# One more Strassen pair in each feed-forward block, the row of 1/rms by products with ones, and weights split in the middle of the unit ahead

## The chip, the cores and the metric

The kernel runs on one core of a Trainium2 chip. The metric is device time in microseconds (us) of one execution; of several executions the median is given. The core has five engines with a queue each: TensorE (PE in the profile; PEld is its weight load), VectorE (DVE), ScalarE (ACT), GpSimd (POOL) and SyncE (SP), which here only issues transfers. Each engine works its queue in order and waits on semaphores for the others.

## The reference

The reference is a two-layer encoder trunk on 512 tokens of 1024 values, in float32. Each layer is a pre-norm attention block and a pre-norm SwiGLU feed-forward block with 2816 inner values:

```python
def rmsnorm(x, g):
    y = x32 * lax.rsqrt(jnp.mean(x32 * x32, axis=-1, keepdims=True) + RMS_EPS)
    return (y * g.astype(jnp.float32)).astype(x.dtype)
...
def swiglu(h, w_gate, w_up, w_down):
    return (jax.nn.silu(h @ w_gate) * (h @ w_up)) @ w_down
...
for i in range(DEPTH):
    h = rmsnorm(x, norm_mix[i])
    x = x + (window_gqa_sink(...) if i % 2 == 0 else dilated_mixture_attention(...))
    h = rmsnorm(x, norm_ffn[i])
    x = x + swiglu(h, w_gate[i], w_up[i], w_down[i])
return rmsnorm(x, norm_final)
```

Layer 0 has windowed attention with grouped queries and a sink logit, layer 1 dilated attention in three groups.

## The kernel before

The activations lie transposed in SBUF: `x` is eight tiles of 128 features by 512 tokens. A float32 product is made of three products of a rounded type (float32r): each operand is split into a high part (a copy that rounds, on ScalarE, `wh`, `xh`) and a low part (the difference, on VectorE, `wl`, `xl`), and `mm3` adds high x high, high x low and low x high into a PSUM bank. A *unit* is 128 output features: eight steps j of six products of 128x256, 48 in all. Its weights come in one transfer of 512 KB and are split by `load` (L104 to L108); three buffers of weights are in flight.

The norm isn't applied to the inputs of a unit. The products run on `x` times the gain, and 1/rms of each token is multiplied in when a result leaves PSUM. The sum of squares (`ssum`) is gathered tile by tile on GpSimd (L273). Then `norm_sums` (L296) adds it over the partitions with four products with a column of ones (`ssq`), and root, reciprocal and one Newton step run on a tile of 128x4 (`norm_columns`); `norm_rows` (L305) turns the result into a row of 512 that is the same in all partitions (`rrow`, four transposes) and copies it to `rb`.

In layer 0 (L345 to L493) attention units are woven with the units of q, k and the output projection by `fill`, a chain of generators: a unit there begins by loading and splitting its own weights, and its products follow.

The feed-forward block `swiglu` (L586) has 22 pairs of units, gate f and up f. The first `plain` of them (six) are ordinary units, in `conventional` (L863). `gated(f)` (L616) scales gate by `rb` and takes Silu, `combined(f)` scales up and multiplies, `kept(f)` splits the result for the down projection. The other pairs are *Strassen pairs*: gate and up of one pair, with the tokens in two halves and the features in two halves, form a 2x2 by 2x2 block product that is done with seven products of half the length (`strassen`, L717), each of 12 products of 128x256. They need seven inputs, normed and then added and subtracted, as high and low parts (`bh`, `bl`), and seven weights. The inputs are made by the 19 steps of `input_steps` (L633): eight `normed`, then `parts` (a split: ScalarE, then VectorE) and `less` (a difference on VectorE). `conventional` calls these steps one by one between the units of the plain pairs; their last pair also makes the weights of the first Strassen pair (`weights`, L681: h12, l12, f5 and so on). In `strassens` (L767) the Strassen pairs follow each other in turns of seven; between the products stand the copies (L726) that take a partial result out of a bank before more is added to it.

Who sets the order: TensorE's queue is in the order of the program text everywhere; in `conventional` and `strassens` (under `manual_schedule` with `ORDERED`) so are those of VectorE and ScalarE. Elsewhere a scheduler orders the other engines when the program is built.

Of the kernel before, what the change touches and what calls it, by code (L numbers as in the profile page):

```python
# [9 lines left out]
F32 = mybir.dt.float32  # L10
# [4 lines left out]
S = 512  # L15
# [51 lines left out]
def trunk(ctx, tc, xT, gains, sink, tabs, qsc, wunits, wv, outT, outR):  # L67
# [85 lines left out]
    def run(gen):  # L153
        for _ in gen:
            pass

    def chain(*gens):
        for _, g in gens:
            yield from g
# [18 lines left out]
    def lined_up(*makers):  # L178
# [5 lines left out]
        for k in range(len(makers)):  # L184
            n, gen = gens[k]
            for c in range(n):
# [3 lines left out]
                    next(gens[-1][1])  # L190
                yield

    def last_outputs(out_part, at, fill=()):

        gens = [out_part(j, at, NK)[1] for j in range(3)]
        for j in range(NK):
            run(gens[j])
            if j + 3 < NK:
                gens.append(out_part(j + 3, 0, NK, ahead=True)[1])
                next(gens[-1])  # L200
            if j == 0:
                run(fill)
# [102 lines left out]
    def norm_rows(blocks=range(4), at=0):  # L305

        r = norm["r"]
        pr = bank("tp", "rrow")
        for b in blocks:
            nc.tensor.transpose(pr[:, 128 * b:128 * b + 128], r[:, at + b:at + b + 1].to_broadcast([128, 128]), ident)  # L310
        rb = norm["rb"] = spool.tile([128, S], F32, name="rb", bufs=1)
        cols = slice(128 * blocks[0], 128 * blocks[-1] + 128)
        nc.scalar.activation(rb[:, cols], pr[:, cols], AF.Copy)
        for done in norm["wait"] or ():
            done()
        norm["wait"] = None
# [32 lines left out]
    with tc.tile_pool(name="l0", bufs=2) as pool:  # L349
# [121 lines left out]
        def out_part(j, lo, hi, w={}, ahead=False):  # L471
            def gen():
# [6 lines left out]
                for c in range(lo, hi):  # L479
                    mm3(out_ps[j], wh[:, c], wl[:, c], oh[:, c, :], ol[:, c, :], c == 0, c == NK - 1)  # L480
                    if c == NK - 1:
# [4 lines left out]

        early = values(0, 0, xh, xl, v0, "ov sc tp mm")[1]
        spread([norm_sums, 4, norm_rows], early)
        fill = chain((16, early), q_unit(0, 2), q_unit(0, 3), k_unit(1),
                     *[q_unit(1, i) for i in range(4)],  # L490
                     *[out_part(j, 0, 4) for j in range(3)], *[out_part(j, 4, 6) for j in range(3)])

        counts = [6, 7, 6, 5, 5, 5, 4, 4, 4, 4, 3, 2, 2, 2, 3, 2]  # L493
        units = [attention0(P, h, b) for P in range(2) for h in range(2) for b in range(4)]
# [90 lines left out]
    def swiglu(u, n):  # L585
        with tc.tile_pool(name="ffn", bufs=2) as pool:  # L586
# [24 lines left out]
            def up(f):  # L611
                def done(ps):
                    part["u"] = ps
                return unit(u0 + 2 * f + 1, xh, xl, ("tp", "mm")[f % 2], done)
# [238 lines left out]
                return (raws.pop(f), *sums_of.pop(f))  # L853

            ORDERED = {mybir.EngineType.PE, mybir.EngineType.DVE, mybir.EngineType.Activation}
            plain = 6
            parts = PARTS[n // 4]
            run(gate(0)[1])
            norm_sums()
            run(up(0)[1])  # L860
            steps = input_steps()

            def conventional():  # L863

                def products(ps, w):
                    for j in range(NK):
                        mm3(ps, w[0][:, j], w[1][:, j], xh[:, j, :], xl[:, j, :], j == 0, j == NK - 1)
                        yield

                def make(m):  # L870
                    for _ in range(m):
                        if steps:
                            steps.pop(0)()

                w = load_unit(wunits[u0 + 2], (NK, 128))
                for f in range(1, plain):
                    g = bank(("mm", "sc")[f % 2])
                    gen = products(g, w)
                    for q in range(4):
                        next(gen), next(gen)  # L880
                        if q == 0:
                            w = load_unit(wunits[u0 + 2 * f + 1], (NK, 128))
                            if f == 1:
                                norm_rows()
                                gated(0)
                            combined(f - 1)
                            part["g"] = g
                        elif q == 2 and f <= 3:
                            kept(f - 1)
                        elif q:  # L890
                            make(1)
                    ps = bank(("tp", "mm")[f % 2])
                    gen = products(ps, w)
                    for q in range(4):
                        if q < 3 or f < plain - 1:
                            next(gen), next(gen)
                        if f == plain - 1:
                            if q == 0:
                                first, parts_ = weights(*ready(f + 1))
                                ahead(f + 2)  # L900
                            for m in (("h12", "l12", "f5"), ("h64", "l64", "f7"), ("h57", "l57"), ("h3", "l3"))[q]:
                                parts_[m]()
                        if q == 3 and plain - 3 <= f < plain - 1:
                            ahead(f + 3, raw=False)
                        if q == 0 and f + 1 < plain:
                            w = load_unit(wunits[u0 + 2 * f + 2], (NK, 128))
                        if q == 0:
                            gated(f)
                        else:
                            make(2 if q == 2 and f < 3 else 1)  # L910
                    part["u"] = ps
                make(len(steps))
                return first, gen
# [505 lines left out]
```

## Time and profile before

| | us |
| --- | --- |
| median of 3 runs (lowest, highest) | 1396.22 (1395.93, 1396.76) |
| profiled execution | 1396.07 |
| its span, first to last instruction | 1394.3 |
| PE busy, x12414 | 1382.5 |
| DVE busy, x1593 | 855.4 |
| ACT busy, x1250 | 681.9 |
| POOL busy, x318 | 225.2 |

The mean granted clock of TensorE is 0.998. The first feed-forward block begins its gate 0 near 182 us, its Strassen pairs at 247.87; the second repeats it some 862 us later. In the profile a row of a time line is start, duration, engine, line, operation, what it writes and reads, shape and count; in brackets the idle time before it and what ended that. Products overlap in TensorE, so that the duration of one is longer than the distance between two.

### The profile page before, as it was taken

How to read it: one execution, taken by the hardware profiler on the slowest of the kernel's cores; microseconds unless marked ns; L12 is line 12 of the kernel's file. 1: busy time of each engine (PE TensorE's matmuls, PEld its weight loads, DVE VectorE, ACT ScalarE, POOL GpSimd, SP SyncE). 2: the span in 40 equal slices, each digit the busy share in tenths (PEclk: the TensorE clock that was granted, in tenths of full speed). 3: DMA queues.
4: the chain of work that ended last, by engine and by line, in shares of the span. 5: the costliest groups of instructions: out<-in, count | busy, mean ns of one | idle time of the engine just before them, and what ended most of it. 6: DMA issues, size and time to landing. Idle time of an engine off the chain costs nothing.

```text
span 1394.3 us, 29677 instructions
## 1 busy us (share of the span) xinstructions
PE 1382.5 (99%) x12414; PEld 1367.2 (98%) x12414; DVE 855.4 (61%) x1593; ACT 681.9 (49%) x1250; POOL 225.2 (16%) x318
## 2 busy tenths in 40 slices
PE   9999999999999999999999999999999999999998
PEld 8988999999999999999999999999999999999998
DVE  6876558853687456345656556646466884388633
ACT  6866534632556356435545436436354462265522
POOL 1233320100110111011112111211132010021022
PEclk9999999999999999999999999999999999999999
DMA  6110263752683232322122222222136383387122
GB/s 203 61 62 16 77 184 104 188 138 99 183 201 92 89 110 94 107 77 92 62 93 80 73 92 76 78 83 71 62 110 179 112 212 105 106 210 194 65 95 73
DMA packets 61063, 153.63 MB, mean 110 GB/s; under 512 B 8320, under 2 KB 14336, under 8 KB 60928
## 3 DMA queue, kind: packets, MB, share of 16 engines
q1 hardware_dynamic: 49888, 134.28, 29.1%
q0 software_dynamic: 10752, 16.92, 7.6%
q8 instruction: 97, 1.59, 0.5%
q10 hardware_dynamic: 288, 0.52, 0.1%
q14 instruction: 38, 0.31, 0.1%
HBM read 149.52 MB, written 2.17 MB: 109 GB/s over the span
## 4 chain that ended last, share of the span: by engine, by line
PE 93%; DVE 3%; ACT 2%; issue 1%; SPq 0%; DMA 0%; POOL 0%; DVEq 0%; ACTq 0%
PE mm L126 38%; PE mm L714 12%; PE sc L126 11%; PE psv L126 9%; PE sc L714 9%; PE tp L126 5%; PE ov L431 1%; PE sc L1140 1%; PE ovb L1195 1%; PE sc L1081 1%; PE tp L1103 1%; ACT pr L407 1%; PE ov L1122 1%; DVE pr L400 1%; PE sc L148 1%; DVE wl L98 1%
## 5 line engine op out<-in xcount | busy, mean ns | idle before, releaser
L98 DVE TENSOR_TENSOR wl<-wraw,wh 128x1024 fp32r<-128x1024 f32 (+5 forms) x196 | 211.6, 1084 | 193.3 <-ACT wh L97 190.4
L97 ACT ACTIVATE wh<-wraw 128x1024 fp32r<-128x1024 f32 (+3 forms) x195 | 181.6, 937 | 240.4 <-PE mm L126 132.2
L126 PE MATMUL mm<-xh,wh 128*128 128x256 f32 x1320 | 267.2, 282 | 0.6 <-ACT xh L259 0.6
L126 PE MATMUL mm<-xl,wh 128*128 128x256 f32 x1320 | 260.9, 278 | 0.1
L126 PE MATMUL mm<-xh,wl 128*128 128x256 f32 x1320 | 260.5, 277 | 0.0
L126 PEld LDWEIGHTS mm<-xh,wh 128*128 128x128 f32 x1320 | 201.6, 189 | 2.5 <-ACT xh L259 0.9
L126 PEld LDWEIGHTS mm<-xl,wh 128*128 128x128 f32 x1320 | 201.0, 189 | 0.7 <-DVE xl L260 0.6
L126 PEld LDWEIGHTS mm<-xh,wl 128*128 128x128 f32 x1320 | 200.8, 189 | 0.0
L671 POOL DMA_DIRECT2D w<-wunits x64 | 56.1, 907 | 417.8 <-DVE wl L694 165.9
L126 PE MATMUL psv<-wh,xh 128*128 128x256 f32 x288 | 80.7, 280 | 0.0
L126 PE MATMUL psv<-wl,xh 128*128 128x256 f32 x288 | 79.9, 277 | 0.2 <-DVE wl L98 0.2
L126 PE MATMUL psv<-wh,xl 128*128 128x256 f32 x288 | 79.8, 277 | 0.0
L273 POOL TENSOR_TENSOR ssum<-ssum,tmp 128x512 f32<-128x512 f32 x26 | 45.8, 1762 | 180.3 <-ACT tmp L270 118.8
L714 PE MATMUL mm<-bh,wh 128*128 128x256 f32 x256 | 70.7, 276 | 0.0
L714 PE MATMUL mm<-bl,wh 128*128 128x256 f32 x256 | 70.7, 276 | 0.0
L714 PE MATMUL mm<-bh,wl 128*128 128x256 f32 x256 | 70.7, 276 | 0.0
L714 PE MATMUL sc<-bh,wh 128*128 128x256 f32 x256 | 70.7, 276 | 0.0
L714 PE MATMUL sc<-bl,wh 128*128 128x256 f32 x256 | 70.7, 276 | 0.0
L714 PE MATMUL sc<-bh,wl 128*128 128x256 f32 x256 | 70.7, 276 | 0.0
L714 PE MATMUL mm<-bh,h 128*128 128x256 f32 x256 | 70.7, 276 | 0.0
L714 PE MATMUL mm<-bl,h 128*128 128x256 f32 x256 | 70.7, 276 | 0.0
L714 PE MATMUL mm<-bh,l 128*128 128x256 f32 x256 | 70.7, 276 | 0.0
(242 smaller groups left out, 3716.0 us busy)
## 6 DMA issues: line engine op xcount, KB each, us to landing
wraw<-wunits SPq DMA_DIRECT2D x159, 512.0 KB, 3.2
w<-wunits SPq DMA_DIRECT2D x96, 256.0 KB, 4.9
w<-wunits POOLq DMA_DIRECT2D x64, 256.0 KB, 5.7
wraw<-wv SPq DMA_DIRECT2D x25, 512.0 KB, 3.3
wraw<-wunits SPq DMA_DIRECT2D x28, 192.0 KB, 2.4
x<-xT SPq DMA_DIRECT2D x8, 256.0 KB, 5.2
wraw<-wunits SPq DMA_DIRECT2D x3, 256.0 KB, 5.8
wraw<-wunits SPq DMA_DIRECT2D x2, 384.0 KB, 2.9
```

The source lines that it names most:

```text
L97: nc.scalar.activation(out_h, src, AF.Copy)
L98: nc.vector.tensor_tensor(out_l, src, out_h.bitcast(F32), op=OP.subtract)
L126: nc.tensor.matmul(out[:, cols], a, b[:, cols], start=first and k == 0 and c == 0, stop=last and k == 2, skip_group_check=True)
L148: nc.tensor.matmul(outs[a], qp[a][:, qc], k[a][:, kc], start=first and k is kp, stop=k is low, skip_group_check=True)
L273: eng.tensor_tensor(norm["sum"], norm["sum"], sq, op=OP.add)
L400: nc.vector.tensor_tensor_reduce(out=pr[:, e, :w], in0=ps[hf], in1=tab0[:, off:off + w], scale=SLOPES[heads[e]], scalar=-3e38, op0=OP.add, ...
L407: nc.scalar.activation(pr[:, e, :w + 1], pr[:, e, :w + 1], AF.Exp, bias=m[:, 1, e:e + 1], accum_out=m[:, 2, e:e + 1])
L431: nc.tensor.matmul(ov[64 * hf:64 * hf + 64, 256 * n:256 * n + 256], v0[:, k0 // 128 + kb, vs], st["pt", kb][:, 256 * hf:256 * hf + 256], s ...
L671: nc.gpsimd.dma_start(sums[:, 512 * k:512 * k + 512], v[:, 0:512], accum_op=OP.add)
L714: nc.tensor.matmul(out, a[:, j], b[:, j], start=first and j == 0 and i == 0, stop=j == 3 and i == 2, skip_group_check=True)
L1081: nc.tensor.matmul(out, qk["qs", p][a][:, 128 * t:128 * t + 128], kp[k], start=t == ts[0] and k == 0, stop=k == 1, skip_group_check=True)
L1103: nc.tensor.transpose(tp[:, (nb * a + kb) * 128:(nb * a + kb) * 128 + 128], st["pr", p, ts][:, a, o + 128 * kb:o + 128 * kb + 128], ident)
```

## The change

Three things, the second and third in both feed-forward blocks.

In layer 0 the units of the chain are driven by a new function `staggered`: when a unit is half done, the next unit is begun, which loads and splits its weights (`ahead=True`); its products come when the first is through.

In the feed-forward blocks `norm_sums` and `norm_rows` give way to `norm_direct`. The sum of squares itself is split, and four products with a 128x128 tile of ones put the sum over partitions into all rows of a bank at once. The root, the reciprocal and the Newton step then run on 128x512, where they ran on 128x4, and give `rb` without a transpose. The products stand after the first step of up 0; the first plain pair's scaling (`gated(0)`) and the first input step follow in the text.

And `plain` is five: pairs 0 to 4 are plain, 5 to 21 Strassen (17, not 16). The 19 input steps and the first Strassen pair's weights then have four plain pairs behind pair 0, not five; the result of pair 2 is split after the plain stage.

```diff
+    def staggered(n, gen, makers):
+        for make in (*makers, None):
+            for c in range(n):
+                if c == n // 2 and make:
+                    after = make()
+                    next(after[1])
+                next(gen)
+                yield
+            if make:
+                n, gen = after
...
+    def norm_direct(pool, between):
+        ones_r = pool.tile([128, 512], F32R, name="l3")[:, 0:128]
+        nc.vector.tensor_scalar(ones_r, ident, 0.0, 1.0, op0=OP.mult, op1=OP.add)
+        parts = [pool.tile([128, 512], F32R, name="h3") for _ in range(2)]
+        split(*parts, norm["sum"])
+        between()
+        ps = bank("tp", "rrow")
+        for k, part in enumerate(parts):
+            for c in range(0, S, 256):
+                nc.tensor.matmul(ps[:, c:c + 256], ones_r, part[:, c:c + 256], start=k == 0 and c == 0, stop=k == 1,
+                                 skip_group_check=True)
+        rb = norm["rb"] = spool.tile([128, S], F32, name="rb", bufs=1)
+        v, t = [pool.tile([128, S], F32, name="us", bufs=4) for _ in range(2)]
+        nc.vector.tensor_scalar(v, ps, 1.0 / D, EPS, op0=OP.mult, op1=OP.add)
+        nc.scalar.activation(rb, v, AF.Sqrt)
+        nc.vector.reciprocal(rb, rb)
+        nc.vector.scalar_tensor_tensor(t, rb, -0.5, rb, op0=OP.mult, op1=OP.mult)
+        nc.vector.tensor_tensor(t, t, v, op=OP.mult)
+        nc.vector.scalar_tensor_tensor(rb, t, 1.5, rb, op0=OP.add, op1=OP.mult)
...
-        fill = chain((16, early), q_unit(0, 2), q_unit(0, 3), k_unit(1),
-                     *[q_unit(1, i) for i in range(4)],
-                     *[out_part(j, 0, 4) for j in range(3)], *[out_part(j, 4, 6) for j in range(3)])
+        makers = [lambda i=i: q_unit(0, i, ahead=True) for i in (2, 3)] + [lambda: k_unit(1, ahead=True)]
+        makers += [lambda i=i: q_unit(1, i, ahead=True) for i in range(4)]
+        makers += [lambda j=j: out_part(j, 0, 4, ahead=True) for j in range(3)]
+        fill = chain((0, staggered(12, early, makers)), *[out_part(j, 4, 6) for j in range(3)])
...
-            plain = 6
+            plain = 5
             parts = PARTS[n // 4]
             run(gate(0)[1])
-            norm_sums()
-            run(up(0)[1])
+            first_up = up(0)[1]
+            norm_direct(pool, lambda: next(first_up))
+            for _ in range(3):
+                next(first_up)
             steps = input_steps()
+            gated(0)
+            steps.pop(0)()
+            run(first_up)
...
-                            if f == 1:
-                                norm_rows()
-                                gated(0)
                             combined(f - 1)
                             part["g"] = g
-                        elif q == 2 and f <= 3:
+                        elif q == 2 and f <= plain - 3:
                             kept(f - 1)
```

In the built program the queues of all five engines are the same, instruction for instruction, from the start through layer 0 to the last product of gate 0 (TensorE) or to the first instruction of the new norm.

TensorE at the start of the first feed-forward block, before (`mm` is the bank of gate 0, `tp` of up 0, `ssum` the sum of squares):

```order
L126 MATMUL mm<-xh,wl 128x256 x2
L277 MATMUL ssq<-ones,ssum 128x1 x4
L126 MATMUL tp<-xh,wh 128x256 x2
L126 MATMUL tp<-xl,wh 128x256 x2
L126 MATMUL tp<-xh,wl 128x256 x2
```

and after (`h_2412`, `h_2413` are the two parts of the sum, `l_2410` the tile of ones):

```order
L126 MATMUL mm<-xh,wl 128x256 x2
L126 MATMUL tp<-xh,wh 128x256 x2
L126 MATMUL tp<-xl,wh 128x256 x2
L126 MATMUL tp<-xh,wl 128x256 x2
L342 MATMUL rrow<-h_2412,l_2410 128x256 x2
L342 MATMUL rrow<-h_2413,l_2410 128x256 x2
```

The four small products between gate 0 and up 0 are gone, as are the four transposes inside gate 1; four ordinary products stand after the first step of up 0.

VectorE in the same place, before (`var`, `rstd` and `newton` are the norm's small tiles, `gs` gate's result, `us` up's, L643 the first input step):

```order
L289 TENSOR_SCALAR var<-ssq 128x4
L98 TENSOR_TENSOR wl<-wraw,wh 128x1024
L291 RECIPROCAL rstd<-rstd 128x4
L292 SCALAR_TENSOR_TENSOR newton<-rstd 128x4
L293 TENSOR_TENSOR newton<-newton,var 128x4
L294 SCALAR_TENSOR_TENSOR rstd<-newton,rstd 128x4
L618 TENSOR_TENSOR gs<-mm,rb 128x512
L623 TENSOR_TENSOR us<-tp,rb 128x512
L624 TENSOR_TENSOR us<-us,gs 128x512
L643 SCALAR_TENSOR_TENSOR h_2531<-x,g_sb,rb 128x256
```

and after:

```order
L98 TENSOR_TENSOR h_2413<-ssum,h_2412 128x512
L98 TENSOR_TENSOR wl<-wraw,wh 128x1024
L346 TENSOR_SCALAR us<-rrow 128x512
L348 RECIPROCAL rb<-rb 128x512
L349 SCALAR_TENSOR_TENSOR us<-rb 128x512
L350 TENSOR_TENSOR us<-us 128x512
L351 SCALAR_TENSOR_TENSOR rb<-us,rb 128x512
L657 TENSOR_TENSOR gs<-mm,rb 128x512
L682 SCALAR_TENSOR_TENSOR h_2464<-x,g_sb,rb 128x256
L682 SCALAR_TENSOR_TENSOR l_2466<-x,g_sb,rb 128x256
L662 TENSOR_TENSOR us<-tp,rb 128x512
```

The five operations of the norm have 512 elements a partition where they had four, and one input step (two rows of L682) stands ahead of the scaling of up 0.

VectorE from the scaling of the last plain gate but one to that of the last, before (L98 with `bl` and L650, L652 are input steps, L98 with `wl` weight splits of plain units, L694 and L700 weights of the first Strassen pair):

```order
L618 TENSOR_TENSOR gs<-mm,rb 128x512
L98 TENSOR_TENSOR wl<-wraw,wh 128x1024
L623 TENSOR_TENSOR us<-tp,rb 128x512
L624 TENSOR_TENSOR us<-us,gs 128x512
L694 TENSOR_TENSOR wl<-wraw,wh 128x1024
L700 TENSOR_TENSOR w_3098<-w_2884,wraw 128x512
L618 TENSOR_TENSOR gs<-sc,rb 128x512
```

and after:

```order
L657 TENSOR_TENSOR gs<-sc,rb 128x512
L689 SCALAR_TENSOR_TENSOR h_2464<-h_2464,h_2612 128x1024
L98 TENSOR_TENSOR bl<-h_2464,bh 128x1024
L98 TENSOR_TENSOR bl<-l_2614,bh 128x1024
L98 TENSOR_TENSOR wl<-wraw,wh 128x1024
L662 TENSOR_TENSOR us<-mm,rb 128x512
L663 TENSOR_TENSOR us<-us,gs 128x512
L733 TENSOR_TENSOR wl<-wraw,wh 128x1024
L739 TENSOR_TENSOR w_2979<-w_2759,wraw 128x512
L657 TENSOR_TENSOR gs<-mm,rb 128x512
```

The last three input operations stood one pair away from the last plain gate; they now stand directly ahead of it.

More of the change, by code (lines that the diff above doesn't have):

```diff
@@ L313, in norm_rows @@
         nc.scalar.activation(rb[:, cols], pr[:, cols], AF.Copy)
+        for done in norm["wait"] or ():
+            done()
+        norm["wait"] = None
+    def norm_direct(pool, between):
[17 more added lines that the diff above has]
+        nc.vector.scalar_tensor_tensor(rb, t, 1.5, rb, op0=OP.add, op1=OP.mult)
         for done in norm["wait"] or ():
```

## Prediction

> **What bounds the kernel now.** I read the page first (busy shares, chain of waits), then the list of what TensorE waited for, then the time lines of TensorE, VectorE and ScalarE around the start of the first feed-forward block.
>
> ```profile
> span 1394.3 us, 29677 instructions
> PE 1382.5 (99%) x12414; PEld 1367.2 (98%) x12414; DVE 855.4 (61%) x1593; ACT 681.9 (49%) x1250; POOL 225.2 (16%) x318
> PE 93%; DVE 3%; ACT 2%; issue 1%; SPq 0%; DMA 0%; POOL 0%; DVEq 0%; ACTq 0%
> ...
> PE sc L148 <- DVE mst L400: 2.7, 2, 2.4
> PE psv L126 <- DVE wl L98: 0.2, 1, 0.2
> ```
>
> The first line under the span is busy time by engine, the second the shares of the chain that ended last; the last two, from the list of waits, who TensorE (PE) waited for, in us, times, longest. TensorE is 93% of the chain and waits for almost nothing. So every product taken away counts in full, provided that nothing new makes TensorE wait. The 61% of VectorE (DVE) is a mean, and the stage that the change shortens is far above it:
>
> ```profile
> 200.30:247.80 47.50, 47.50 (x422) 47.50 (x421) 40.66 (x54) 21.02 (x25) 0.00 (x0) 1.00 0.31 97
> ```
>
> This row is the stretch of the plain pairs in the first feed-forward block: length, then busy time of PE, PEld, DVE, ACT, POOL. VectorE works 40.66 of 47.50 us here.
>
> **The change part by part.** *Layer 0.* In the built programs the queues of all five engines hold the same instructions with the same waits, from the start to the last product of gate 0: weights were already split where the scheduler had room. So this part costs and brings nothing; had it acted, the weights' whole wait is the 0.2 us quoted.
>
> *Products of the norm.* Before, four products with a column of ones (ssq) and four transposes (rrow) stand in TensorE's queue:
>
> ```profile
> 187.77 0.95 PE L277 MATMUL ssq<-ones,ssum 128*128 128x1 f32 x8
> 188.58 0.48 PE L126 MATMUL tp<-xh,wh 128*128 128x256 f32 x2
> 188.90 0.40 PE L126 MATMUL tp<-xl,wh 128*128 128x256 f32 x2
> ...
> 195.73 0.60 PE L310 MATMUL rrow<-ident,rstd 128*128 128x128 f32 x4
> 196.09 0.49 PE L126 MATMUL sc<-xh,wh 128*128 128x256 f32 x2
> ...
> 200.26 0.39 PE L126 MATMUL mm<-xh,wh 128*128 128x256 f32 x2
> ...
> 1049.37 0.95 PE L277 MATMUL ssq<-ones,ssum 128*128 128x1 f32 x8
> ```
>
> First column: start, second: duration of the row, xN: products in it. Starts, not durations, give the pace, since products overlap: the chain rows below have 96 in 10.88 us, 0.1133 each, while the 58 from 188.90 to 195.73 take 0.1178 each. From 187.77 to 200.26 TensorE does 96 products of 128x256 (up 0 and gate 1) in 12.49 us. The change does the 96 and four more of the same form and type: 100 x 0.1133 = 11.33. That is **-1.16 us** for each block; it includes the slower pace behind ssq, which I take to go with it (if it stays: 58 x 0.0045, 0.26 less gain).
>
> *Five plain pairs.* A plain pair is 96 products, a Strassen pair 7 x 12 = 84:
>
> ```profile
> 200.43 10.88 PE mm L126 x96
> ...
> 258.91 2.72 PE mm L714 x24
> ...
> 268.43 2.72 PE mm L714 x24
> ```
>
> In the chain of waits, 96 products take 10.88 us; a Strassen pair returns after 268.43 - 258.91 = 9.52. That is **-1.36 us** for each block. Without any new wait both blocks give 2 x 2.52 = 5.0 us.
>
> *The new chain of the norm.* Its split needs the sum of squares:
>
> ```profile
> 184.65 1.79 POOL L273 TENSOR_TENSOR ssum<-ssum,tmp 128x512 f32<-128x512 f32 x1 [3.65 <-ACT tmp L270]
> 188.84 1.23 DVE L98 TENSOR_TENSOR wl<-wraw,wh 128x1024 fp32r<-128x1024 f32 x1
> 188.82 1.28 ACT L290 ACT_TABLE_LOAD   x1
> 197.07 0.69 DVE L618 TENSOR_TENSOR gs<-mm,rb 128x512 f32<-128x512 f32 x1 [5.95 <-ACT rb L313]
> 198.28 0.63 ACT L619 ACTIVATE gs<-gs 128x512 f32<-128x512 f32 x1
> ```
>
> The sum ends at 186.44, ScalarE's half of the split (0.63, as the last row) at 187.1, VectorE's (0.69) at 187.8; TensorE wants them after six products, at 187.77 + 0.68 = 188.45. Nothing waits, with 0.6 us to spare. Then VectorE is in the weight split until 190.0 (what follows one starts 1.13 after it, as 206.65 and 207.78 below). Its first step on the row reads PSUM, 0.75 us by the row of L579 below: 190.75. The root takes 0.63: 191.4, its table being loaded by 190.1. Then the reciprocal, now 128x512, a size the trace doesn't have:
>
> ```profile
> L579 DVE TENSOR_SCALAR wraw<-turned,rstd 128x512 f32<-128x512 f32 x2 | 1.4, 748 | 0.1
> L409 DVE RECIPROCAL mst<-mst 128x2 f32<-128x2 f32 x32 | 5.2, 164 | 13.2 <-ACT pr L407 12.8
> L1165 DVE RECIPROCAL mb<-mb 128x4 f32<-128x4 f32 x16 | 2.9, 179 | 0.5
> ...
> L291 DVE RECIPROCAL rstd<-rstd 128x2 f32<-128x2 f32 x2 | 0.3, 167 | 0.5 <-ACT rstd L290 0.5
> L291 DVE RECIPROCAL rstd<-rstd 128x8 f32<-128x8 f32 x1 | 0.2, 193 | 0.0
> ```
>
> These are groups by form; after the bar busy us and mean ns of one. On one line, six more elements cost 193 - 167 = 26 ns, 4.3 ns each: 0.167 + 510 x 0.0043 = **2.4 us**, which I take, as both ends stand on the same line. The low end is another 128x512 operation, 0.69. The high end is the steepest slope, (179 - 164)/2 = 7.5 ns between L409 and L1165: 4.0 us. A page speaks against even the middle: the Trainium skill, "VectorE: DVE Perf Modes", section "First, the fixed hardware budget", has the reciprocal run by an iterated divide with a repeat count of 8. [...]
>
> With 2.4 the reciprocal ends at 193.8. Three dependent steps follow, 0.72 apart like the middle two here:
>
> ```profile
> 206.65 1.22 DVE L98 TENSOR_TENSOR wl<-wraw,wh 128x1024 fp32r<-128x1024 f32 x1
> 207.78 0.68 DVE L623 TENSOR_TENSOR us<-mm,rb 128x512 f32<-128x512 f32 x1
> 208.50 0.69 DVE L624 TENSOR_TENSOR us<-us,gs 128x512 f32<-128x512 f32 x1
> 209.11 0.48 DVE L643 SCALAR_TENSOR_TENSOR h<-x,g_sb,rb 128x256 f32<-128x256 f32 x1
> ```
>
> so gate 0 is scaled (L618) at 196.0, not 197.07: 1.07 earlier on the clock, about level with TensorE, which is 1.16 earlier. Nobody waits for it there: the banks that it frees are wanted only by up 2 and up 3.
>
> *VectorE with one pair less.* Behind it stand, in one queue, the weight splits, the 19 steps that make the Strassen pairs' inputs, and the combining of the pairs. The steps all remain; a plain pair takes only six operations with it, by the spacing of the rows just shown: the scaling of gate and of up and their product (0.61 + 0.72 + 0.61), two weight splits (2 x 1.13), and one split of a result that moves behind the stage (0.61): 4.8 us. TensorE's time for the stage shrinks by 10.88. So 40.66 - 4.8 = 35.9 us of work face 47.50 - 10.88 = 36.6 us, and VectorE also stands still inside the steps, because each split waits for ScalarE's half:
>
> ```profile
> 198.94 0.69 DVE L624 TENSOR_TENSOR us<-us,gs 128x512 f32<-128x512 f32 x1 [0.59 <-ACT gs L619]
> 214.83 1.23 DVE L98 TENSOR_TENSOR bl<-h,bh 128x1024 fp32r<-128x1024 f32 x1 [1.71 <-ACT bh L97]
> 224.40 1.23 DVE L98 TENSOR_TENSOR bl<-h,bh 128x1024 fp32r<-128x1024 f32 x1 [0.53 <-ACT bh L97]
> 229.62 1.23 DVE L98 TENSOR_TENSOR bl<-l,bh 128x1024 fp32r<-128x1024 f32 x1 [1.13 <-ACT bh L97]
> 240.10 1.23 DVE L98 TENSOR_TENSOR wl<-wraw,wh 128x1024 fp32r<-128x1024 f32 x1 [1.65 <-ACT wh L97]
> 244.31 0.68 DVE L618 TENSOR_TENSOR gs<-sc,rb 128x512 f32<-128x512 f32 x1
> 250.51 0.37 ACT L726 ACTIVATE gs<-mm 128x256 f32<-128x256 f32 x1
> 257.81 0.37 ACT L726 ACTIVATE us<-mm 128x256 f32<-128x256 f32 x1
> ```
>
> In brackets: idle before the row and what ended it. The last plain gate is scaled at 244.31, that is 47.24 after the first. Of the idle time 0.59 goes (two steps now stand between) and 1.65 goes (a VectorE that is behind finds its weights ready); 1.71 + 0.53 + 1.13 remain. So the last plain gate is scaled at 196.0 + 47.24 - 4.8 - 2.24 = **236.2**. From there a fixed chain runs: Silu, the second weight split of the first Strassen pair, its sums, ScalarE's splits, and behind them in ScalarE's queue the copies of the first products (L726) that must be out before TensorE may add to the same bank. It ends 250.88 - 244.31 = 6.57 and 258.18 - 244.31 = 13.87 later. TensorE's products that wait for them, the third and the sixth of the first Strassen pair:
>
> ```profile
> 251.94 0.28 PE L714 MATMUL mm<-bh,h 128*128 128x256 f32 x1
> ...
> 258.75 0.28 PE L714 MATMUL mm<-bh,h 128*128 128x256 f32 x1
> ```
>
> Both were ready before, by 1.06 and 0.57 us. Now they are wanted 10.88 + 1.16 = 12.04 earlier, at 239.90 and 246.71, and the copies are out at 242.8 and 250.1: TensorE is held 2.9 us, and 3.4 in all. Part of the 2.9 may show already at the weights of up 4, in the same queue. Later Strassen pairs have their old order and pace, so I expect no more.
>
> *Sum.* Each block: -1.16 - 1.36 + 3.36 = +0.84; both, since the second block repeats the first (its ssq at 1049.37): +1.7. The profiled execution took 1396.07 us, 0.15 below the median of the runs: **1397.8 us**, 0.1% slower.
>
> **The rivals.** *The backlog is absorbed.* If TensorE doesn't follow VectorE because the copies slip past, the products alone count: 1396.07 - 5.0 = 1391.0. For it speaks that no wait shows in this stage now; against it the margins of 1.06 and 0.57 us, against a deadline that moves by 12.04. *The reciprocal is cheap,* 0.69 like its neighbours: the chain is 1.7 us shorter for each block, 1397.8 - 3.4 = 1394.4. Against it: the slope on L291 is over three times that of a plain operation of this length (0.69 us over 512 elements, 1.3 ns). *The reciprocal is dear,* 4.0 us at the slope of L409 to L1165, and its extra 1.6 us goes straight through gate 0's scaling to the copies: 1397.8 + 3.2 = 1401.0, slower. It decides from a reciprocal of about 3.0 us, where the sum passes the bound of slower; the sizes measured are tiny ones, which speaks neither way. *The layer-0 part acts after all:* excluded by the identical queues.
>
> **How the numbers follow.** A measurement of this kernel can tell 0.2%, 2.8 us, from no change: faster ends below 1393.4, slower begins above 1399.0. The forecast has 0.55, the cheap reciprocal 0.12, the dear one 0.24, the absorbed backlog 0.09. The likeliest case's own range is 1396.3 to 1399.3 (0.7 us either way for a block), so of its 0.55 some 0.05 lie above 1399.0; the cheap case keeps 0.02 beyond the bound of faster. Faster 0.11, same 0.60, slower 0.29. The range takes in the cheap and the dear reciprocal with what a measurement scatters: 1394.0 to 1401.3.
>
> **What would show it.** All rows up to about 187.8 us at the same times; the new rrow products near 188.45 with no wait; RECIPROCAL 128x512 at 2.4 us; the scaling of gate 0 near 196.0; VectorE without idle time but for its waits on ScalarE until the Strassen pairs; in TensorE's list a new wait of 2 to 3 us in front of the third product of the first Strassen pair and a smaller one in front of its sixth, twice in the program. A TensorE without such waits would prove me wrong towards 1391; a reciprocal of 4 us, or waits in later pairs too, towards 1401.

## The result and the profile after

The changed kernel takes **1400.92 us** (median of 7 executions, 1399.10 to 1401.26) against 1396.76 before (7, 1395.93 to 1398.35): ratio 1.0028, 95% interval 1.0019 to 1.0037, so slower by a little more than a measurement tells from no change. The profiled execution took 1399.57 us. The prediction was 1397.8 with a range of 1394.0 to 1401.3.

The page of the profile after: span, busy time by engine, and the chain that ended last by engine.

```profile
span 1397.8 us, 29644 instructions
PE 1381.0 (99%) x12374; PEld 1363.8 (98%) x12374; DVE 872.3 (62%) x1607; ACT 687.5 (49%) x1260; POOL 227.8 (16%) x322
PE 85%; DVE 8%; ACT 4%; issue 2%; SPq 0%; DMA 0%; POOL 0%; DVEq 0%; ACTq 0%
```

TensorE does 40 products fewer, as planned, but VectorE now has 8% of the chain, not 3%. The list of what TensorE waited for (us in total, times, longest) has the waits at which the chain goes over to VectorE and ScalarE:

```profile
PE mm L753 <- ACT gs L765: 2.8, 2, 1.6
...
PE mm L126 <- DVE wl L98: 0.6, 1, 0.6
...
PE tp L126 <- DVE wl L98: 0.4, 1, 0.4
...
PE mm L753 <- ACT us L765: 0.2, 1, 0.2
```

L765 is the copy that was L726. These waits stand where the prediction had put them, at the copies of the first Strassen pair and at the weights of up 4, and in the second block also at those of gate 4. The time lines of VectorE, ScalarE and TensorE in the first block, in this order:

```profile
189.86 3.35 DVE L348 RECIPROCAL rb<-rb 128x512 f32<-128x512 f32 x1 [0.70 <-ACT rb L347]
...
195.43 0.69 DVE L657 TENSOR_TENSOR gs<-mm,rb 128x512 f32<-128x512 f32 x1
...
235.35 0.68 DVE L657 TENSOR_TENSOR gs<-mm,rb 128x512 f32<-128x512 f32 x1
```

```profile
241.55 0.36 ACT L765 ACTIVATE gs<-mm 128x256 f32<-128x256 f32 x1
...
248.85 0.36 ACT L765 ACTIVATE us<-mm 128x256 f32<-128x256 f32 x1
```

```profile
240.02 0.39 PE L126 MATMUL tp<-xh,wl 128*128 128x256 f32 x2
241.96 0.38 PE L753 MATMUL mm<-bh,h 128*128 128x256 f32 x1 [1.55 <-ACT gs L765]
```

The wide reciprocal takes 3.35 us, gate 0 is scaled at 195.43 and the last plain gate at 235.35; TensorE stands still until the copy is out at 241.91.

A second thing isn't in any list of waits. These rows are stretches of the first block, of before and then of after: length, busy time of PE and PEld with the number of instructions, then DVE, ACT, POOL, the granted clock, DMA share and GB/s.

```profile
200.00:230.00 30.00, 30.00 (x267) 30.00 (x267) 26.53 (x39) 13.72 (x17) 0.00 (x0) 1.00 0.34 102
300.00:400.00 100.00, 100.00 (x885) 100.00 (x884) 57.08 (x75) 39.97 (x58) 8.75 (x10) 1.00 0.52 147
```

```profile
200.00:230.00 30.00, 30.00 (x257) 30.00 (x256) 26.82 (x35) 13.53 (x16) 0.00 (x0) 1.00 0.29 92
300.00:400.00 100.00, 100.00 (x884) 100.00 (x884) 57.01 (x75) 39.96 (x58) 8.73 (x10) 1.00 0.52 147
```

TensorE is busy without a gap in all four, at the full clock, yet in the plain pairs (200 to 230) it does 257 products in place of 267. The distances of their starts are 0.1178 us there and 0.1133 otherwise. It is the slower pace that the prediction saw for 58 products behind ssq. Here it begins at the new products of rrow and lasts 380 products, to the next wait, one of 0.1 us at the weights of up 4.

From the starts in the two traces the time can be put together, counted from TensorE's first product. A block is counted from the end of gate 0 to the first product of layer 1 (first block) or to TensorE's last product (second block):

| | before | after | difference |
| --- | --- | --- | --- |
| layer 0, to the end of gate 0 | 186.40 | 184.90 | -1.50 |
| first block | 346.15 | 347.81 | +1.66 |
| layer 1, to the end of its gate 0 | 515.45 | 516.84 | +1.39 |
| second block | 338.60 | 340.27 | +1.67 |

The first row isn't the change. Ahead of a wait of 2.4 us for attention the two executions are 0.04 us apart. Behind it the one of before ran at about half the clock for some 3 us, the one of after did not, and from there on they are 1.48 us apart:

```profile
100.50:104.00 3.50, 3.08 (x12) 3.08 (x13) 2.92 (x12) 1.31 (x4) 0.26 (x1) 0.56 0.27 108
```

```profile
100.50:104.00 3.50, 3.12 (x24) 2.49 (x26) 2.75 (x12) 1.92 (x6) 0.31 (x1) 1.00 0.23 92
```

The third figure from the end is the granted clock, 0.56 and 1.00. The Trainium skill, "TensorE: Matmul & The Clock Gate", section "Part 1: The HAM clock gate", says that activity is judged in a window that runs freely, so that the same kernel meets it at another point each time; the two executions agree with that. The third row of the table is the slower pace again, in the output projection of layer 1, where some of the later executions have it too. What the change costs is 1.66 and 1.67 us in its two blocks.

### The profile page after: what moved, and what is told of

The parts are those of the page before. It is cut to its first block, busy times and chain, and to the rows that moved or that the text cites. A ratio compares the mean times of both kernels' runs of the same rounds, so it can differ in the third digit from the quotient of the medians.

```text
span 1397.8 us, 29644 instructions
## 1 busy us (share of the span) xinstructions
PE 1381.0 (99%) x12374; PEld 1363.8 (98%) x12374; DVE 872.3 (62%) x1607; ACT 687.5 (49%) x1260; POOL 227.8 (16%) x322
## 3 DMA queue, kind: packets, MB, share of 16 engines
HBM read 151.10 MB, written 2.17 MB: 110 GB/s over the span
## 4 chain that ended last, share of the span: by engine, by line
PE 85%; DVE 8%; ACT 4%; issue 2%; SPq 0%; DMA 0%; POOL 0%; DVEq 0%; ACTq 0%
PE mm L126 34%; PE mm L753 13%; PE sc L753 10%; PE psv L126 9%; PE sc L126 8%; PE tp L126 2%; DVE wl L98 2%; PE ov L469 1%; PE sc L1181 1%; PE ovb L1236 1%; PE sc L1122 1%; PE tp L1144 1%; ACT pr L445 1%; DVE bl L98 1%; PE ov L1163 1%
## 5 line engine op out<-in xcount | busy, mean ns | idle before, releaser
L98 DVE TENSOR_TENSOR wl<-wraw,wh 128x1024 fp32r<-128x1024 f32 (+4 forms) x192 | 207.1, 1083 | 192.6 <-ACT wh L97 189.6
L97 ACT ACTIVATE wh<-wraw 128x1024 fp32r<-128x1024 f32 (+5 forms) x191 | 177.4, 935 | 236.7 <-PE mm L126 126.0
L126 PE MATMUL mm<-xh,wh 128*128 128x256 f32 x1288 | 260.6, 282 | 0.9 <-ACT xh L272 0.5
L126 PE MATMUL mm<-xh,wl 128*128 128x256 f32 x1288 | 254.3, 277 | 0.6 <-DVE wl L98 0.6
L126 PE MATMUL mm<-xl,wh 128*128 128x256 f32 x1288 | 254.3, 277 | 0.6 <-DVE xl L273 0.6
L126 PEld LDWEIGHTS mm<-xh,wh 128*128 128x128 f32 x1288 | 195.9, 188 | 3.2 <-ACT xh L272 0.9
L126 PEld LDWEIGHTS mm<-xl,wh 128*128 128x128 f32 x1288 | 195.7, 188 | 1.0 <-DVE xl L273 1.0
L126 PEld LDWEIGHTS mm<-xh,wl 128*128 128x128 f32 x1288 | 195.5, 188 | 1.0 <-DVE wl L98 0.9
L753 PE MATMUL mm<-bh,h 128*128 128x256 f32 x272 | 75.5, 278 | 3.0 <-ACT gs L765 2.8
L753 PE MATMUL mm<-bh,wh 128*128 128x256 f32 x272 | 75.1, 276 | 0.0
```

The source lines that it names most:

```text
L97: nc.scalar.activation(out_h, src, AF.Copy)
L98: nc.vector.tensor_tensor(out_l, src, out_h.bitcast(F32), op=OP.subtract)
L126: nc.tensor.matmul(out[:, cols], a, b[:, cols], start=first and k == 0 and c == 0, stop=last and k == 2, skip_group_check=True)
L753: nc.tensor.matmul(out, a[:, j], b[:, j], start=first and j == 0 and i == 0, stop=j == 3 and i == 2, skip_group_check=True)
```

## The experiments

The theory of the holds: VectorE's backlog keeps TensorE waiting, and the reciprocal sizes it. The rival, formed from the trace after: the pace, which the products of rrow or a wait can turn over, and which then stays until the next disturbance. The table is read from the starts of all products in the trace of each kernel. *Block* is the block's length less that of before, *slow* what the pace of 0.1178 costs in it (before: 0.29 and 0.50), *held* the gaps of 0.13 us and more between products of 128x256, less 0.1133 each (before: 0.27 and 0.44).

| kernel | block 1 | slow | held | block 2 | slow | held | executions, us |
| --- | --- | --- | --- | --- | --- | --- | --- |
| changed, first | +1.66 | 2.05 | 2.26 | +1.67 | 0.84 | 3.84 | 7: 1399.1 to 1401.3 |
| e0 | +1.68 | 2.04 | 2.29 | +11.92 | 12.55 | 2.48 | 5: 1398.5 to 1402.7; 6: 1409.9 to 1413.7 |
| e1 | +0.70 | 0.13 | 1.84 | +0.69 | 1.97 | 0.39 | 9: 1397.2 to 1399.4; 2: 1409.5, 1412.0 |
| e2 | +15.70 | 11.38 | 6.33 | +4.92 | 1.06 | 6.16 | 4: 1406.1 to 1407.1; 2: 1418.6, 1419.8 |
| e3 | +10.82 | 13.47 | 0.09 | +10.19 | 13.03 | 0.26 | 2: 1395.9, 1397.0; 6: 1406.0 to 1407.5; 4: 1415.9 to 1418.0 |
| e4 | +2.13 | 1.79 | 2.63 | +12.31 | 12.29 | 2.77 | 4: 1409.5 to 1412.1 |
| e5 | +1.66 | 0.13 | 3.81 | +1.70 | 0.56 | 3.79 | 2: 1399.7, 1399.8; 4: 1409.9 to 1412.5 |
| e6 | +10.82 | 13.47 | 0.09 | -2.10 | 0.32 | 0.59 | 3: 1404.2 to 1406.2; 3: 1417.1 to 1417.4 |
| e7 | -1.81 | 0.29 | 0.18 | +10.28 | 12.67 | 0.35 | 9: 1391.2 to 1393.9; 3: 1405.6 to 1406.7 |
| e8 | -1.81 | 0.30 | 0.18 | -1.80 | 0.51 | 0.35 | 5: 1391.6 to 1392.6 |
| e9 | +2.12 | 1.80 | 2.61 | +2.15 | 2.00 | 2.83 | 10: 1399.0 to 1401.1 |
| e10 | +11.38 | 12.02 | 1.38 | -0.20 | 0.73 | 1.37 | 5: 1394.9 to 1397.8; 7: 1407.4 to 1408.8 |
| e11 | +2.17 | 0.92 | 3.18 | +2.15 | 0.77 | 3.69 | 5: 1399.5 to 1402.6 |

The kernel before, run beside e0 to e3, e4 to e7, e8 and e9, e10 and e11, has medians of 1397.31, 1396.17, 1396.18 and 1395.97 and no execution outside 1394.3 to 1399.6. The kernels e0 to e3 ran on one chip, e4 to e7 on a second, e8 to e11 on a third. The times of most others lie in groups 10 to 13 us apart. In every traced execution of an upper group one block, or both, runs at the slower pace to its end; for the executions without a trace this is inferred.

**e0: the changed kernel once more.**

> The changed kernel unaltered, profiled a second time, as the reference of the other runs. In its first trace two things stand against the 5.0 us that the missing products bring: holds of TensorE by ScalarE's copies and weights (2.3 us in the first feed-forward block, 3.6 in the second), and stretches in which products follow each other at 0.1178 us instead of 0.1133 (380 + 47 products in the first block, 325 ahead of and 90 in the second, 1.9 us each). Theory of the holds: they repeat within 0.2 us. Theory of the pace: if the stretches are set by the program they stand at the same places, from the products of rrow to the next wait in the first block, and the time is 1400 to 1401; if they are set by accidents of time they stand elsewhere, and the time differs by up to 2 us either way.

In the first block the holds and the stretch behind rrow repeat. The second is entered at 0.1133 here, at 0.1178 in the first trace; rrow turns it to the slower pace, and the holds are 2.48 us where they were 3.84. And TensorE comes out of its last hold there at the slower pace, and keeps it:

```profile
300.00:400.00 100.00, 100.00 (x885) 100.00 (x884) 57.01 (x75) 39.86 (x57) 8.73 (x10) 1.00 0.50 143
1150.00:1250.00 100.00, 100.00 (x851) 100.00 (x850) 50.16 (x68) 35.13 (x51) 7.00 (x8) 1.00 0.45 132
```

851 products in 100 us where the first block does 885, both at the full clock. Six of eleven executions lie in the upper group; in the first seven there was none. The median of the eleven is 1409.89 us, ratio 1.0068 (1.0041 to 1.0095). So the first median is that of the lower group, and the change is worse than it says. That the spread would be at most 2 us was wrong.

**e1: the direct norm with six plain pairs.** Edit: `-plain = 5`, `+plain = 6`.

> The direct norm with six plain pairs, so without the shorter stage. Theory of the holds (VectorE's backlog in the shorter stage makes them): VectorE has one pair more of room, gate 0 is scaled as early as before, and the products save 1.16 us in each block less at most 0.5 of hold: 1 to 2.3 us faster than before. Theory of the pace (the products of rrow put TensorE into the slow pace until its next wait): with no wait behind it the slow pace lasts for most of the first block, some 2900 products at 0.0045 us: up to 13 us slower than before. Rival that the wide reciprocal by itself makes TensorE wait: holds of 1 us and more in front of the first Strassen pair here too.

```profile
PE tp L126 <- DVE wl L98: 0.7, 1, 0.7
PE tp L126 <- ACT wh L97: 0.5, 1, 0.5
```

The lower group (median 1398.46) is 1.15 us slower than before, where the theory of the holds had a gain: one pair more of room isn't enough. In the first block 1.7 us of waits stand at the weights of up 4. In the second the plain pairs run at the slower pace, 1.5 us of it more than before, and TensorE comes late enough to wait 0.1. Both blocks end at +0.7. VectorE's split of the weights of up 4, in the first block of before and then of e1, here with the row ahead of it:

```profile
231.90 1.22 DVE L98 TENSOR_TENSOR wl<-wraw,wh 128x1024 fp32r<-128x1024 f32 x1
```

```profile
232.47 1.23 DVE L98 TENSOR_TENSOR bl<-h,bh 128x1024 fp32r<-128x1024 f32 x1 [1.13 <-ACT bh L97]
233.61 1.22 DVE L98 TENSOR_TENSOR wl<-wraw,wh 128x1024 fp32r<-128x1024 f32 x1
```

Counted from the end of gate 0 (187.77 and 188.75) that is 44.1 us before and 44.9 in e1. The new norm has gate 0 scaled after 9.1 us, the old one after 9.3: next to nothing is gained there, as its five operations on VectorE take 6.1 us (0.68, 3.35 and three of 0.69) where the old ones were on 128x4. And one more split of the inputs, the row above, stands ahead of these weights, because the input steps begin one step earlier. TensorE, with its fewer products, gets to up 4 1.1 us earlier. So the rival was right that holds come without the shorter stage, at another place than it said; how much of them is the reciprocal's, e1 doesn't separate.

**e2: five plain pairs with the old norm.** Edit: the kernel before with `-plain = 6`, `+plain = 5`, and `f <= plain - 3` for the pairs whose result is split at once.

> The kernel before with five plain pairs and its old norm (products with a column of ones, reciprocal on 128x8 and 128x2, transposes). Theory of the holds: gate 0 is scaled at the old time and the Strassen pair is wanted 10.9 us earlier, so the copies hold TensorE for 3.4 to 3.9 us in each block against 1.36 saved: 4 to 5 us slower than before. If the holds come from the wide reciprocal alone, there are none here, and it is 2.7 us faster. Theory of the pace: the old transposes leave TensorE at 0.1133 until the first hold; behind each hold either pace may follow.

```profile
PE mm L714 <- ACT gs L726: 3.5, 2, 2.4
...
PE tp L126 <- ACT wh L97: 2.4, 2, 1.2
PE tp L126 <- DVE wl L98: 1.4, 2, 0.7
```

Here the holds are largest, without a wide reciprocal (the old one is on 128x4): 5.7 us more than before in the second block. In the first the long waits are followed by 5 us at a mean clock of 0.66, which is in its 6.33. The lower group is 9.5 us slower than before, twice the size expected. VectorE's scaling of the first and the last plain gate in its first block:

```profile
197.08 0.69 DVE L618 TENSOR_TENSOR gs<-mm,rb 128x512 f32<-128x512 f32 x1 [5.70 <-ACT rb L313]
...
240.11 0.68 DVE L618 TENSOR_TENSOR gs<-mm,rb 128x512 f32<-128x512 f32 x1
```

They are 43.03 us apart, in the changed kernel 39.92. In between VectorE stands still for ScalarE 6.2 us here (0.59, 1.71, 1.13, 1.65, 1.12) and 3.1 there (0.26, 0.57, 1.12, 1.12): that is the whole difference of 3.1 us. The steps stand one place earlier in the queue of the changed kernel, which would change how often a split finds ScalarE's half ready; no run moves the steps alone. So the shorter stage makes holds with the old norm too, as the new norm does without the shorter stage in e1.

**e3: a constant in place of the reciprocal.** Edit: `-nc.vector.reciprocal(rb, rb)`, `+nc.vector.tensor_scalar(rb, rb, 0.0, 0.05, op0=OP.mult, op1=OP.add)`.

> The changed kernel with a constant in place of the reciprocal, written by a plain operation on 128x512 (0.69 us): the reciprocal of the root is left out, all else stays. Theory of the holds: the chain to the copies is 2.7 us shorter; the holds fall to about 0.3 us in the first block and 1 in the second, 4 to 5 us faster than the changed kernel, as fast as before or a little faster. Theory of the pace: with the holds gone nothing resets the slow pace that starts at the products of rrow, and up to 13 us of the slow pace come in place of the holds. If the reciprocal lies beside other work, the time is that of the changed kernel.

No hold is left in either block; the row of L765 is gone from the list of waits. And nothing ends the slower pace that begins at rrow, some 3000 and 2900 products:

```profile
300.00:400.00 100.00, 100.00 (x851) 100.00 (x851) 53.88 (x71) 38.08 (x54) 8.70 (x10) 1.00 0.49 139
1150.00:1250.00 100.00, 100.00 (x852) 100.00 (x851) 49.37 (x66) 34.49 (x51) 6.83 (x8) 1.00 0.43 124
```

Less the slower pace beyond that of before, the blocks are 10.82 - 13.18 = -2.36 and 10.19 - 12.53 = -2.34, where the prediction's -2.52 without the 0.26 us of slower pace in it is -2.26. Both theories hold: the saving is there, the holds hide it, and the pace costs more than either.

**e4 and e5: transposes to set the pace.** Edit of e4, behind the sixth product of the first Strassen pair; e5 has the same four in gate 1, at the place of the old rrow, into rrow's bank.

```diff
+                    if f == plain:
+                        for b in (2, 3, 2, 3):
+                            nc.tensor.transpose(v["a"][:, 128 * b:128 * b + 128], ident, ident)
```

> The changed kernel with four fp32 transposes of a constant tile behind the sixth product of the first Strassen pair of each block, where the last hold is over; their result is not used. Old rrow transposes of this form were followed by the pace of 0.1133 us in all four cases traced in a feed-forward block. Theory of the pace (whichever pace TensorE takes after its last hold stays for some 2400 products, 11 to 12 us): the upper cluster of times of the changed kernel, 1410 to 1414, is gone, and all runs lie at 1399.5 to 1403, the lower cluster and 0.5 us a block for the transposes. Rival that something else made those runs long: two clusters stay, 10 us apart.

> The changed kernel with the same four transposes in gate 1 instead, where those of rrow stood before, so that the plain pairs run at 0.1133 us. Theory of the holds: TensorE reaches the waits about 1.5 us earlier in each block and waits longer by that, so the holds grow from 2.3 to 3.5 to 4 us and the time does not fall: 1400 to 1403 in the lower cluster. Theory of the pace: what follows the last hold is left to chance as in the changed kernel, so an upper cluster 11 to 13 us higher remains. If the slow pace alone costs the time, the lower cluster falls by 2 to 3 us.

e4 fell: all four executions lie in the upper group. In the first block of its trace the pace is 0.1133 on both sides of the transposes, in the second 0.1133 ahead and 0.1178 behind. Such transposes aren't a reset; nor are they of the old form, which takes a column repeated and not the tile ident. e5 went as the theory of the holds said: with the plain pairs at 0.1133 the holds are 3.8 us, and the blocks last as long as in the changed kernel, to 0.03 us. Its waits, with the copy now at L766:

```profile
PE mm L754 <- ACT gs L766: 3.1, 2, 1.6
...
PE tp L126 <- DVE wl L98: 1.3, 2, 0.6
...
PE mm L754 <- ACT us L766: 0.5, 2, 0.2
```

In the lower group slow pace and holds trade one for one: TensorE arrives with VectorE, whichever way it comes.

**e6 and e7: no holds.** Edit of e6: the reciprocal goes to ScalarE, and the first Strassen pair's weights are split in another order. e7 adds e5's transposes.

```diff
-        nc.scalar.activation(rb, v, AF.Sqrt)
-        nc.vector.reciprocal(rb, rb)
+        nc.scalar.activation(rb, v, AF.Ln)
+        nc.scalar.activation(rb, rb, AF.Exp, scale=-0.5)
...
-for m in (("h12", "l12", "f5"), ("h64", "l64", "f7"), ("h57", "l57"), ("h3", "l3"))[q]:
+for m in (("h12", "l12", "f5", "h64"), ("f7", "h57", "l64"), ("l57", "h3"), ("l3",))[q]:
```

> The changed kernel with the reciprocal of the root computed as exp(-ln(v)/2) on ScalarE, ahead of the same Newton step, and with the weight splits of the first Strassen pair in another order (ScalarE's half of pieces 6 and 4 ahead of the last Silu, the sums for 5 and 7 together). By the waits traced so far the copies are out 4 us earlier. Theory of the holds: no hold is left. Theory of the pace: the products of rrow turn the pace over, nothing turns it back, and each block that entered at 0.1133 runs at 0.1178 to its end, about 13 us: single runs at 1391 to 1393, 1404 to 1406 or 1417 to 1419. If the pace is no matter of the program, all runs lie at 1391 to 1394.

> e6_no_holds and the four fp32 transposes in gate 1 of each block. Theory of holds and pace together: no hold, the pace is 0.1133 from the transposes to the end of each block in every run, and the products saved count: 1396.8 - 5.0 + 0.9 = 1392.7, between 1392 and 1394.5, 3 to 4 us faster than before, all runs in one cluster. If holds return at the faster pace, up to 2 us more in a block and a second cluster.

The holds are gone, 0.6 us at most. In e6 each block shows what rrow does alone: the first, entered at 0.1133, runs at 0.1178 to its end; the second, entered at 0.1178, runs at 0.1133 and is 2.10 us shorter than before:

```profile
300.00:400.00 100.00, 100.00 (x852) 100.00 (x851) 54.22 (x72) 39.07 (x55) 8.72 (x10) 1.00 0.50 140
1150.00:1250.00 100.00, 100.00 (x885) 100.00 (x884) 52.69 (x71) 36.29 (x53) 7.01 (x8) 1.00 0.48 136
```

In e7 nine of twelve executions lie at 1391.2 to 1393.9, the gain that was expected, and three 13 us higher; in the traced one the transposes of the second block turned 0.1133 into 0.1178.

**e8 and e9: transposes of the old form.** Edit against e7 (e9: against e4): the transposes take a column repeated 128 times.

```diff
-nc.tensor.transpose(norm["again"][:, 128 * b:128 * b + 128], ident, ident)
+nc.tensor.transpose(norm["again"][:, 128 * b:128 * b + 128], g_sb[:, 0, b:b + 1].to_broadcast([128, 128]), ident)
```

> e7_no_holds_reset with one thing changed: the four transposes in gate 1 take a column repeated 128 times, as the old rrow transposes did, in place of the tile ident. Behind the old ones the second product started 206 to 207 ns after the first and the pace was 0.1133 in every case traced; behind those of ident the second product starts after 201 ns and the pace was 0.1133 twice and 0.1178 once in the two runs with them in gate 1. Theory: the form of the transpose decides what pace follows; with the old form there is no hold and no slow block in any run, all runs lie at 1391 to 1394, 3 to 4 us faster than before. Rival: the pace behind transposes is chance whatever their form, and about a quarter of the runs lie at 1403 to 1407 as for e7_no_holds_reset.

> e4_reset_after_holds with the same replacement: transposes of a repeated column behind the sixth product of the first Strassen pair. Theory that the form decides: the pace is 0.1133 from there to the end of each block in every run, 1399.5 to 1403, no run above 1405. Rival that it is chance, or that the place in the order decides: runs at 1409 to 1412 as in e4_reset_after_holds.

e8 is faster than both kernels: **1392.21 us** (1391.64 to 1392.58), ratio to before 0.9968, interval 0.9956 to 0.9981. The three stretches of its trace have the faster pace throughout:

```profile
200.00:230.00 30.00, 30.00 (x267) 30.00 (x266) 26.81 (x34) 14.55 (x17) 0.00 (x0) 1.00 0.29 95
300.00:400.00 100.00, 100.00 (x884) 100.00 (x884) 57.77 (x76) 41.22 (x59) 9.59 (x11) 1.00 0.55 154
1150.00:1250.00 100.00, 100.00 (x885) 100.00 (x884) 54.89 (x74) 38.81 (x56) 7.51 (x9) 1.00 0.49 142
```

e9 is the changed kernel in its lower group in all ten executions (1400.57, ratio 1.0027, 1.0018 to 1.0037), where e4, with the other form and on another chip, had all four in the upper. The sign named in the expectation fell in one half: in e8 the second product behind the transposes starts after 201 to 202 ns, as behind those of ident, and the pace is 0.1133 all the same. The other half stands: where it started after 206 to 207 ns, 0.1133 followed in all eight cases traced, after 201 to 202 ns in 11 of 14.

**e10 and e11: reciprocal and order priced.** Both have the old form in both places. e10 is e8 with Sqrt and reciprocal back, e11 also with the old order of the weight splits.

> e8_no_holds_broadcast with the reciprocal on 128x512 put back (Sqrt, then 3.35 us on VectorE), and transposes of the repeated column in gate 1 and behind the sixth product of the first Strassen pair, so that the pace is 0.1133 in every run whatever waits there are. It prices the reciprocal alone. Theory of the holds: the chain to the copies is 1.5 us longer than with exp and ln; holds of 0.9 to 1.5 us come back in each block; with 0.45 a block for the added transposes 1394.5 to 1396.5. Rival that the earlier weight splits alone removed the holds: 1393.1.

> The changed kernel with its own reciprocal and its own order of weight splits, and the same two groups of transposes. It prices the order of the weight splits against e10_reciprocal_back, and the holds of the change at the faster pace: 3.5 to 4 us in each block, as in e5_reset_after_rrow, 1399.5 to 1401.5 in one cluster. If the order of the splits is no matter, the time is that of e10_reciprocal_back.

In e10 holds of 1.2 and 1.0 us come back beyond e8's, all at units of the plain pairs; the lower group is 1396.82, 0.85 above before. In the second blocks, which stay at the faster pace, the order of the splits is worth 2.15 + 0.20 = 2.35 us (e11 against e10), and the reciprocal 1.80 - 0.20 = 1.60 (e10 against e8), 0.45 of it for the added transposes. And e10 shows the limit of the transposes, against the expectation that the pace would be 0.1133 in every run. In its first block TensorE reached the second group at 0.1178 and left it at 0.1178; seven of twelve executions ended in the upper group:

```profile
300.00:400.00 100.00, 100.00 (x851) 100.00 (x851) 53.29 (x71) 38.09 (x54) 8.22 (x10) 1.00 0.49 138
```

Transposes of a repeated column were followed by 0.1133 in 10 of 10 cases traced in gate 1 (those of the kernel before and of e2 among them) and in 5 of 6 behind the holds; those of ident in 4 of 6. In four of those 5 cases behind the holds the pace was 0.1133 ahead of the transposes already. That the form matters is likely, but not shown: e9 and e4, and e8 and e7, ran on different chips, and five executions of e8 say little against the three slow ones of twelve in e7. On the chip of e4 and e7 only the kernel before has repeated columns; none of its 17 executions lies in an upper group, but ahead of its transposes stand the products of ssq and not those of rrow. The form doesn't decide alone, as e10 shows, and what does is open.

## Why the prediction was right or wrong

The time fell inside the range, but not in the case held likeliest: 0.28% slower had a chance of 0.29, no change 0.60. That it fell inside is in part luck: none of the first seven executions lies in the upper group, and the median of the eleven of e0, 1409.89, is far outside.

*Layer 0* was right: no wait and no instruction of the change shows there, and the -1.50 us of the traced pair is the clock.

*The products* were right. e3, without its slower pace, and e6's second block (-2.10, with 0.59 held) show them within 0.1 to 0.4 us a block.

*The new chain of the norm* failed in one term: the reciprocal, taken at 2.4 us from the slope on L291, measured 3.35. The range of 0.69 to 4.0 held it. By the prediction's own working each further us goes straight through, 2 x 0.95 = 1.9: 1397.8 + 1.9 = 1399.7. The profiled execution took 1399.57. So close a match is chance, since layer 0 gave 1.50 us and layer 1 took 1.39 that the prediction hadn't foreseen; block by block the working has 0.84 + 0.95 = +1.79, the trace +1.66 and +1.67. What came is the rival of the dear reciprocal, said to decide from about 3.0 us. The Trainium skill, "VectorE: DVE Perf Modes", section "First, the fixed hardware budget", has the reciprocal run with a repeat count of 8. The trace agrees in so far as it takes 3.35 us where its neighbours of the same size take 0.69.

*The chain to the copies* was right. Moved by the 1.50 us of layer 0, and with 0.95 for the reciprocal, it had the last plain gate at 235.65 and the copies out at 242.25 and 249.55; they came at 235.35, 241.91 and 249.21.

*The holds* were right in cause and place. With the dearer reciprocal the working has 3.36 + 0.95 = 4.31 us a block; measured were 2.0 and 3.4 more than before. The step behind the difference is the pace. The prediction let the slower pace go with ssq and gave 0.26 us if it stayed for the 58 products. In fact rrow's own products brought it on in the first block, for almost the whole of the plain pairs, and slow products cost 1.8 us more there than before. TensorE came later, and waited less by as much; e5 shows the two as one sum. In the second block, entered at the slower pace, rrow turned it to the faster, and holds and slow pace together are the same again: 1.99 + 1.76 = 3.75 and 3.40 + 0.34 = 3.74, where the working has 4.31 - 0.26 = 4.05. In the first block the copies were out 0.3 us earlier than worked out, which is about the difference.

*Later pairs "have their old order and pace, so I expect no more"* is the step that failed outright. The order was the old one; the pace was not safe. The kernel before has no wait in its 16 pairs, and its pace stays 0.1133 there. The change puts waits ahead of some 2400 products, and behind a wait either pace may follow: 11 to 12 us, more than twice the 5.0 us that the missing products were to bring. By their times, none of the first seven executions has it and six of the eleven of e0 do.

## What to carry to other kernels

Where TensorE runs without a gap, count its products per 100 us as well as its waits: a pace 4% slower shows in no list of waits, and behind a wait of 0.1 us, or a few inserted products, the other pace can follow and stay for 300 us. A stage freed of work on one engine must be reckoned by the engine that then paces it, with the halves of its splits that it waits for: here the order of one pair's weight splits was worth 2.35 us a block, more than the 1.16 us of the products taken out of the norm. And times in separate groups call for more executions and a profile of each group, not for a median, and for two variants to be set side by side on one chip.

## What the runs showed of the hardware

TensorE's float32r products of 128x256 have two steady paces at a full clock, 0.1133 and 0.1178 us, and either can last for 3000 products. The four products of rrow turned the pace over in all 24 cases traced, 19 times to the slower and 5 times to the faster. Nothing in the records tells why. With the slower pace each product takes 0.281 us in place of 0.276, and one weight load in three 0.192 us where all others take 0.187 to 0.188, as with the faster pace; the instructions are the same. The Trainium skill, "TensorE: Matmul & The Clock Gate", section "Back-to-back issue gap", gives one spacing for a form, set by weight load and product together; these runs show two for the same form. Why the faster pace mostly follows transposes of a repeated column, and whether e8 stays at it over many more executions than its five, is open.
